# A diffusion layer with experts: modulation in pairs of column blocks, a branch's transfers on another queue, another order of weight slots

## The chip, the cores and the metric

The kernel runs on one core of one Trainium2 chip. The metric is the device time in microseconds (us) of one execution; lower is better.

## The reference

256 latent tokens `x` and 256 context tokens of width 1024 pass one layer. What is computed, cut to the parts that the change touches:

```python
mod_lat = split(silu(c) @ w_mod + b_mod, 6)         # sh1, sc1, g1, sh2, sc2, g2: 1024 each
mod_ctx = split(silu(c_ctx) @ w_mod + b_mod, 6)     # of these only csh1, csc1 are used
h_lat = modulate(rms_norm(x, norm_mix_g), sh1, sc1) # modulate: h * (1 + scale) + shift
h_ctx = modulate(rms_norm(ctx, norm_mix_g), csh1, csc1)
y = token_mixer(h_lat, h_ctx, ...)   # w_in projections, two linear-attention branches, w_out_a, w_out_b, gates, w_out
x = x + g1 * y
h = modulate(rms_norm(x, norm_ffn_g), sh2, sc2)
x = x + g2 * moe_ffn(h, ...)         # each token in 4 of 32 experts; w_gu (1024x2048) and w_down (1024x1024) of each
return rms_norm(x, final_norm_g)
```

All tensors are 32-bit floats. The experts' weights are 32 x 12 MB and are each read once.

## The kernel before, in words

The work falls into four stages. **The start** computes the first two modulation vectors and the normalized inputs (`hT`, split into a rounded part and its rest, and `hF`, unsplit). **The mixer** runs two orders written out by hand, `ORDER1` and `ORDER2` (lines 34 and 35): each word calls one piece (`K`, `Q`, `V`, `P`: projections, `U`, `X`: gated linear attention, `A`, `I`, `B`: gated delta rule, and so on), and a planner orders the instructions of each engine after its own costs. **The tail** (from line 998) multiplies with the rest of `w_out_a`, with `w_out`, adds the residual and computes the router. **The experts** (from line 1323) run one after the other: each takes 12 chunks of 1 MB, 8 of `w_gu` and 4 of `w_down`.

**The other four modulation vectors** (gate 1, shift 2, scale 2, gate 2) are made during `ORDER1`. Each of its 32 words `M1` calls `wmod_next` (line 889) for one block of 128 columns of `w_mod`: two transfers of 256 KB into a ring of three tiles `wm`, eight matmuls in four column groups (each group sums two of the eight row blocks, on its own 32 partitions of the bank `pm`), a copy `mr` of 128x128 out of the bank (VectorE and ScalarE take turns), and one step later `wmod_sum`: a matmul with `mr` as weights and a column `sum4` sums the four groups into `pc`, and one VectorE instruction adds the bias into a column of `mod2`.

**The chunks of the experts' weights** lie in 21 slots, used in turn (`slots`, `mchunk`, `wload`, lines 927 to 962). Most slots are tiles of earlier stages (`hT0`, `ra`, `hT1`, `yh`, `yT`, `hF`, `yl`, `kA`, `x1`), so a slot's first chunk waits for the last reader of the old tile. `prefetch` issues the first ones: the word `C1` of `ORDER2` one chunk each (three), the tail the numbers in `PF` (4 at its begin, then after each merge and each output block), the latter held back by a tiny GpSimd copy that waits for the step's result. The last three of the first round go through GpSimd's queue; all other chunks through SyncE's, in the order of the program, which carries the weights of all projections too.

**A branch** (`beyond`, line 1290) computes experts that got more than 64 tokens. It stands ahead of expert 12, behind the issue of 20 chunks (line 1349); its body has transfers on SyncE's queue. In this run it isn't taken.

**The last expert** weights its result `pd` by the token's share and the gate (`ys`), splits it into two parts and scatters them with matmuls onto the tokens (`py`); then the final norm follows.

Of the kernel before, what the change touches and what calls it, by code (L numbers as in the profile page):

```python
# [20 lines left out]
KT = 8  # L21
# [8 lines left out]
NB1 = 10  # L30
PF = (4, 0, 2, 0, 0, 1, 1, 0, 1, 0, 2, 1, 0)
DN = (0, 2, 1, 3)
HLB = (2, 2)
ORDER1 = "K0 Pq0 K1 Pk0 M1 U0 Pv0 Pv1 Pq1 Pk1 U1 M1 Pv2 M1 X0 M1 M1 M1 R0 M1 M1 K2 Pk2 Q0 M1 M1 Pq2 R1 M1 Pv4 M1 U2 Pq3 T0 M1 Pv3 X1 M1 M1 V0 Pv6 M1 Pv5 M1 T2 M1 T1 R2 M1 M1 Pk3 U3 V3 M1 V1 M1 Pv7 M1 X2 M1 R4 M1 K3 R3 M1 T3 V2 M1 R5 X3 Q1 Q2 R6 M1 M1 Q3 M1 R7 M1 M1"
ORDER2 = "A0 A0 G0 A0 A0 I0 I0 I0 I0 I0 I0 K4 G1 Z0 I0 K5 G3 Z1 G4 K6 G2 Z2 I0 G5 G6 K7 Z3 B0 B0 B0 B0 B0 B0 A1 T4 Q4 B0 A1 V4 Q6 V5 A1 A1 I1 T6 I1 T7 G7 I1 I1 T5 Z4 I1 I1 V6 H0 Q5 H1 Z5 I1 V7 I1 Q7 H2 Z6 B1 Z7 B1 B1 W0 H3 B1 B1 B1 C1 H4 B1 H5 H6 J0 Y0 Y1 Y2 H7 C1 Y3 C1"


@with_exitstack
def hybrid_layer(ctx, tc, x, c, ctxt, c_ctx, w_mod, b_mod, norm_mix_g, norm_ffn_g, w_in, conv_w, a_log_f, a_log_b,
# [307 lines left out]
    T.transpose(pt, GeT.rearrange("p a h c -> p (a h c)"), ident)  # L347
    Gr = cst.tile([128, 128], F32, name="Gr")
    V.tensor_copy(Gr, pt)
# [537 lines left out]
    wms = [0]  # L887

    def wmod_next(n):

        for _ in range(n):
            k, wms[0] = wms[0], wms[0] + 1
            col = 2048 + 128 * k
            if "pD" in gl_static:
                w = wtake(w_mod, col)
                w = w[:, 0:4], w[:, 4:8]
            else:
                w = [ga.tile([128, 4, 128], F32, tag="wm", bufs=3, name=f"wm{k}{i}") for i in range(2)]
                for i in range(2):
                    nc.sync.dma_start(w[i], w_mod[0][512 * i:512 * i + 512, col:col + 128].rearrange("(k p) n -> p k n", p=128))  # L900

            pt = GD([128, 128], f"pm{k}")
            for kt in range(KT):
                r = 32 * (kt % 4)
                T.matmul(pt[r:r + 32], sc[:, kt], w[kt // 4][:, kt % 4], start=kt < 4, stop=kt >= 4)
            mr = lng.tile([128, 256], F32, tag="sq", bufs=2, name=f"mr{k}")[:, 0:128]
            (S.copy if k % 2 else V.tensor_copy)(mr, pt)
            pend.append((k, mr))
            if k:
                wmod_sum()  # L910
            if k == 31:
                wmod_sum()

    pend = []

    def wmod_sum():
        k, mr = pend.pop(0)
        pc = GD([128, 1], f"pc{k}")
        T.matmul(pc, mr, sum4, start=True, stop=True)
        v_, b = (2, 0, 1, 3)[k // 8], k % 8  # L920
        if v_ == 1:
            V.scalar_tensor_tensor(mod2[:, 1, b:b + 1], pc, b1c[:, b:b + 1], vc[:, 72 + b:73 + b], ALU.add, ALU.mult)
        else:
            V.tensor_add(mod2[:, v_, b:b + 1], pc, vc[:, 40 + k:41 + k])


    slots = [("hT0", 0), ("hT0", 1), (big, "ra")]
    nslot = NB1 + 11
    wide = {}
    nch = [0]  # L930

    def mchunk(name):
        pool, tag = slots[nch[0] % nslot]
        nch[0] += 1
# [8 lines left out]
    def wload(e, wgu, wdn, i, after=None):  # L943

        if (e, i) in pre:
            return pre.pop((e, i))
        w = mchunk(f"w{e}_{i}")

# [3 lines left out]
        if i < 8:  # L952
            q.dma_start(w, wgu[128 * i:128 * i + 128, :])
        else:
            r = 256 * DN[i - 8]
            w3, d3 = w.rearrange("p (k n) -> p k n", k=2), wdn[r:r + 256, :].rearrange("(k p) n -> p k n", p=128)
            if (e, i) == (NE - 1, 11):
                for k in range(2):
                    q.dma_start(w3[:, k], d3[:, k])
            else:  # L960
                q.dma_start(w3, d3)
        return w

    def prefetch(n, after=None):

        for _ in range(min(n, len(slots) - nch[0])):
            e, i = divmod(nch[0], 12)
            pre[e, i] = wload(e, w_gu[0, e], w_down[0, e], i, after)
# [107 lines left out]
    S.dma_start(bf[1], b_down[0])  # L1076
    slots += [(big, "hF"), (mwA, "m0"), (big, "yl"), (big, "kA"), (mo, "x1")]
    prefetch(nslot - nch[0])
# [113 lines left out]
    def ffn(e, xe, wts, sel, places_, mid=None, post=None, late=False, last=False):  # L1192
# [54 lines left out]

        oT, pc = places_()
        ys = wk.tile([128, 512], F32, tag="glu", bufs=1, name=f"ys{e}")
        V.scalar_tensor_tensor(ys, pd, pc, grow, ALU.mult, ALU.mult)  # L1250
# [4 lines left out]
        def scatter():  # L1255
            for t in range(2):
                for a in range(2):
                    for hf in range(2):
                        mm(py[t][:, hf], oT[h_[hf], t], yp[a][h_[hf]], start=False, stop=last and a == 1)
        return scatter  # L1260
# [28 lines left out]

    def beyond():  # L1290
        rd = dr.tile([128, 2, 2, NE], F32, name="rd")
        idd = dr.tile([96, NE], BF16, name="idd")
        vmax = nc.values_load(cnt[0:1, NE:NE + 1], min_val=0, max_val=256)
        with tc.If(vmax > CAP):
            nc.sync.dma_start(rd[:, :, 0], pos)
            nc.sync.dma_start(rd[:, :, 1], pr)
            nc.sync.dma_start(idd, id3)

            def piece(src):
                w = wk.tile([128, 512], F32, tag="sig", bufs=1, name="fw")  # L1300
                nc.sync.dma_start(w, src)
                return w

            with tc.For_i(0, NE, 1) as ev:
                ce = nc.values_load(cnt[0:1, bass.ds(ev, 1)], min_val=0, max_val=256)
                for q in range(1, 4):
                    with tc.If(ce > CAP * q):
                        rc = wk.tile([128, 2, 2], F32, tag="rc", bufs=2, name=f"rc{q}")
                        nc.sync.dma_start(rc[:, :, :, None], rd[:, :, :, bass.ds(ev, 1)])
                        sl = wk.tile([96, 1], BF16, tag="sl", bufs=2, name=f"sl{q}")  # L1310
                        nc.sync.dma_start(sl, idd[:, bass.ds(ev, 1)])
                        V.tensor_scalar_add(rc[:, :, 0], rc[:, :, 0], float(-CAP * q))
# [30 lines left out]
    for e in range(NE):  # L1343
        if e == 12:
# [3 lines left out]

            for i in range(20):
                ec, ic = e + i // 12, i % 12  # L1350
                pre[ec, ic] = wload(ec, w_gu[0, ec], w_down[0, ec], ic)
            beyond()
            quad(e)
            place(e)

        def post(e=e):
# [4 lines left out]
            if e + 1 < NE and e + 1 != 12:  # L1361
                if (e + 1) % 4 == 0:
# [3 lines left out]
                     sc_[0], post, e == 0, e == NE - 1)  # L1366
    sc_[0]()


    fg = mchunk("fg")  # L1370
    nc.sync.dma_start(fg[:, 0:D], dap(final_norm_g, 0, [[0, 128], [1, D]]))
    yo = mchunk("yo").rearrange("p (t n) -> p t n", t=2)
    yg = wk.tile([128, 512], F32, tag="aT", name="yg")
# [39 lines left out]
```

## Time and profile before

| | us |
|---|---|
| median of 3 runs | 1624.34 (1623.12 to 1627.99) |
| the profiled execution | 1624.66 |
| its span, first to last instruction | 1622.8 |
| TensorE busy | 1463.0 (90%) |
| VectorE busy | 652.4 (40%) |
| ScalarE busy | 455.4 (28%) |

Times in the rows are us from the span's start unless marked ns. PE is TensorE's matmul, PEld its weight load, DVE VectorE, ACT ScalarE, POOL GpSimd, SP SyncE; a "q" behind the name means the engine's sequencer (waits, branches, issue of transfers). PEclk is the granted share of TensorE's clock. "L905" is line 905. A 32-bit matmul of the program appears as two instructions.

### The profile page before, as it was taken

How to read it: one execution, taken by the hardware profiler on the slowest of the kernel's cores; microseconds unless marked ns; L12 is line 12 of the kernel's file. 1: busy time of each engine (PE TensorE's matmuls, PEld its weight loads, DVE VectorE, ACT ScalarE, POOL GpSimd, SP SyncE). 2: the span in 40 equal slices, each digit the busy share in tenths (PEclk: the TensorE clock that was granted, in tenths of full speed). 3: DMA queues.
4: the chain of work that ended last, by engine and by line, in shares of the span. 5: the costliest groups of instructions: out<-in, count | busy, mean ns of one | idle time of the engine just before them, and what ended most of it. 6: DMA issues, size and time to landing. Idle time of an engine off the chain costs nothing. (4 is left out here: it accounts for less than half of the span.)

```text
span 1622.8 us, 22690 instructions
## 1 busy us (share of the span) xinstructions
PE 1463.0 (90%) x9150; PEld 812.6 (50%) x9151; DVE 652.4 (40%) x1540; ACT 455.4 (28%) x984; POOL 20.6 (1%) x53
## 2 busy tenths in 40 slices
PE   6999999998998898999999987989889889889886
PEld 2777777877886798633434323323223223223221
DVE  4785676795689776511212111111111111111112
ACT  2655455664365544510101000011001011001001
POOL 2000000000000000000000000000000000000000
PEclk9899999999999999999999999999999999999999
DMA  9437454643333539899999999999999999999997
GB/s 292 133 94 196 116 155 127 166 119 104 104 92 97 191 120 339 274 416 417 415 416 417 414 417 373 416 416 416 416 416 418 415 416 417 415 417 416 415 417 295
DMA packets 221934, 491.82 MB, mean 303 GB/s; under 512 B 13106, under 2 KB 150664, under 8 KB 189024
## 3 DMA queue, kind: packets, MB, share of 16 engines
q1 hardware_dynamic: 220096, 485.86, 79.3%
q0 software_dynamic: 1056, 3.46, 0.6%
q8 instruction: 74, 1.21, 0.3%
q10 hardware_dynamic: 672, 0.99, 0.2%
q14 instruction: 36, 0.29, 0.1%
HBM read 489.15 MB, written 1.11 MB: 302 GB/s over the span
## 5 line engine op out<-in xcount | busy, mean ns | idle before, releaser
L1098 PE MATMUL g<-w,xTm 128*64 128x512 f32 x1616 | 375.1, 599 | 36.7 <-DMA w<-in_w_gu_dram 35.1
L1098 PEld LDWEIGHTS g<-w,xTm 128*64 128x64 f32 x1616 | 105.9, 136 | 281.1 <-issue 166.0
L1220 DVE TENSOR_SCALAR glu<-g 128x256 f32<-128x256 f32 x64 | 24.2, 419 | 464.7 <-PE g L1098 464.7
L1098 PE MATMUL pd<-w,aT 128*64 128x512 f32 x864 | 195.8, 597 | 2.0 <-DMA w<-in_w_down_dram 1.8
L203 PE MATMUL pdin_w_in_dram<-hT,hiin_w_in_dram 128*128 128x512 f32 (+1 forms) x704 | 161.1, 366 | 5.6 <-ACT z L809 3.9
L1221 ACT ACTIVATE sig<-glu 128x256 f32<-128x256 f32 x64 | 23.3, 409 | 501.0 <-DVE glu L1220 501.0
L203 PEld LDWEIGHTS pdin_w_in_dram<-hT,hiin_w_in_dram 128*128 128x128 f32 x704 | 115.4, 190 | 29.0 <-issue 6.7
L1250 DVE SCALAR_TENSOR_TENSOR ys<-pd,pcm,grow 128x512 f32<-128x512 f32 x32 | 24.0, 751 | 255.7 <-PE pd L1098 255.7
L1098 PEld LDWEIGHTS pd<-w,aT 128*64 128x64 f32 x864 | 59.7, 137 | 114.5 <-issue 98.4
L1098 PE MATMUL g<-chT,xTm 128*64 128x512 f32 x432 | 102.4, 600 | 12.7 <-DMA chT<-in_w_gu_dram 11.9
L391 DVE SCALAR_TENSOR_TENSOR ra<-ra,cw 128x192 f32<-128x192 f32 (+2 forms) x192 | 90.3, 474 | 13.7 <-ACT ra L385 11.2
L279 PE MATMUL pfin_w_in_dram<-hF,win_w_in_dram 128*128 128x256 f32 x368 | 90.5, 394 | 0.3 <-ACT tgb L358 0.3
L1252 ACT CAST ysig<-ys 128x512 fp32r<-128x512 f32 x32 | 19.8, 618 | 252.1 <-DVE ys L1250 252.1
L203 PE MATMUL pdin_w_in_dram<-hT,loin_w_in_dram 128*128 128x512 f32 (+1 forms) x352 | 83.2, 367 | 2.2 <-DVE loin_w_in_dram L83 2.2
L279 PEld LDWEIGHTS pfin_w_in_dram<-hF,win_w_in_dram 128*128 128x128 f32 x368 | 70.4, 197 | 12.1 <-issue 1.6
L83 DVE TENSOR_TENSOR loin_w_in_dram<-win_w_in_dram,hiin_w_in_dram 128x1024 fp32r<-128x1024 f32 x49 | 59.6, 1219 | 22.0 <-ACT hiin_w_in_dram L82 21.3
L1098 PEld LDWEIGHTS g<-chT,xTm 128*64 128x64 f32 x432 | 27.9, 136 | 77.0 <-issue 40.7
L203 PEld LDWEIGHTS pdin_w_in_dram<-hT,loin_w_in_dram 128*128 128x128 f32 x352 | 59.1, 190 | 14.3 <-DVE loin_w_in_dram L83 3.2
L1231 PE MATMUL pa<-ident,glu 128*128 128x128 f32 x128 | 26.6, 289 | 39.6 <-DVE glu L1224 38.0
L82 ACT CAST hiin_w_in_dram<-win_w_in_dram 128x1024 fp32r<-128x1024 f32 x49 | 51.2, 1045 | 16.6 <-DMA win_w_in_dram<-in_w_in_dram 11.2
L1098 PE MATMUL pxm<-ohm,xp 128*128 128x256 f32 x256 | 36.1, 297 | 6.1 <-DVE ohm L1139 4.4
L1098 PEld LDWEIGHTS pxm<-ohm,xp 128*128 128x128 f32 x256 | 33.2, 200 | 13.5 <-PE g L1098 4.9
(489 smaller groups left out, 1927.1 us busy)
## 6 DMA issues: line engine op xcount, KB each, us to landing
w<-in_w_gu_dram SPq DMA_DIRECT2D x200, 1024.0 KB, 20.0
w<-in_w_down_dram SPq DMA_DIRECT2D x106, 1024.0 KB, 20.1
chT<-in_w_gu_dram SPq DMA_DIRECT2D x54, 1024.0 KB, 20.0
win_w_in_dram<-in_w_in_dram SPq DMA_DIRECT2D x72, 512.0 KB, 4.0
chT<-in_w_down_dram SPq DMA_DIRECT2D x20, 1024.0 KB, 20.1
wm<-in_w_mod_dram SPq DMA_DIRECT2D x64, 256.0 KB, 3.5
wm<-in_w_mod_dram SPq DMA_DIRECT2D x16, 512.0 KB, 12.6
win_w_out_b_dram<-in_w_out_b_dram SPq DMA_DIRECT2D x8, 512.0 KB, 4.1
```

The source lines that it names most:

```text
L82: S.copy(hi, src)
L83: V.tensor_sub(lo, src, hi)
L203: T.matmul(p if n == 256 else p.rearrange("p (a b) -> p a b", a=2), hl[i][:, kt], r, start=i + a + kt == 0, stop=a == 1 and kt == KT - 1)
L279: T.matmul(p, w[:, kt], act[:, kt], start=kt == 0, stop=kt == KT - 1)
L391: V.scalar_tensor_tensor(al[:, r0:r1], raw[:, r0 + y - 1:r1 + y - 1, x_:x_ + 64], wc(y, x_), al[:, r0:r1], ALU.mult, ALU.add)
L1098: return inorder(T.matmul(*args, **kw))
L1220: V.tensor_scalar_min(gl_[:, cs], pg[0][:, cs], 7.0)
L1221: sig = S.activation(sg_[:, cs], gl_[:, cs], AF.Sigmoid, scale=1.702)
L1231: T.transpose(pt[:, a], gl_[:, 256 * c_ + 128 * a:256 * c_ + 128 * a + 128], ident))
L1250: V.scalar_tensor_tensor(ys, pd, pc, grow, ALU.mult, ALU.mult)
L1252: S.copy(yp[0], ys)
```

## The change

1. `wmod_next` takes two column blocks a call: 16 words `M1` instead of 32, at nearly the same places of `ORDER1` (the one ahead of `U0` goes). Each call has four transfers, 16 matmuls into one bank of 256 columns, one VectorE transpose in blocks of 32x32 out of the bank and a copy of every 32nd column into `modT`. After the last call four matmuls with a wider `sum4` sum all 32 blocks at once, and five VectorE instructions make `mod2`.
2. The slots have another order: `hF` first, then `ra`, then `hT0`; four words `C1` in `ORDER2` instead of three, the first of them earlier; `PF` begins 1, 2, 2 instead of 4, 0, 2.
3. The branch's transfers are issued by GpSimd; ten chunks instead of 20 are issued ahead of it, and the load of the count it compares is tied behind the tenth.
4. The last expert weights, splits and scatters its result in two halves of 256 columns.

```diff
-PF = (4, 0, 2, 0, 0, 1, 1, 0, 1, 0, 2, 1, 0)
+PF = (1, 2, 2, 0, 0, 1, 1, 0, 1, 0, 2, 1, 0)
...
-    sum4 = cst.tile([128, 1], F32, name="sum4")
-    V.tensor_reduce(sum4, ident[:, 0:128:32], AX.X, ALU.add)
+    sum4 = cst.tile([128, 32], F32, name="sum4")
+    V.tensor_reduce(sum4, ident.rearrange("p (g j) -> p j g", g=4), AX.X, ALU.add)
...
+            pt = GD([128, 256], f"pm{k}")
+            for j in range(2):
+                col = 2048 + 256 * k + 128 * j
                 for i in range(2):
+                    w = ga.tile([128, 4, 128], F32, tag="wm", bufs=3, name=f"wm{k}{j}{i}")
+                    nc.sync.dma_start(w, w_mod[0][512 * i:512 * i + 512, col:col + 128].rearrange("(k p) n -> p k n", p=128))
+                    for kt in range(4):
+                        T.matmul(pt[32 * kt:32 * kt + 32, 128 * j:128 * j + 128], sc[:, 4 * i + kt], w[:, kt],
+                                 start=i == 0, stop=i == 1)
+            mr = lng.tile([128, 256], F32, tag="sq", bufs=2, name=f"mr{k}")
+            V.transpose(mr, pt)
+            V.tensor_copy(modT[:, k], mr[:, 0:256:32])
+        if wms[0] == 16:
+            pc = GD([128, 32], "pc")
+            mv = modT.rearrange("p k b -> p (k b)").rearrange("p (b q) -> p q b", q=4)
+            for q in range(4):
+                T.matmul(pc[32 * q:32 * q + 32], sum4, mv[:, q], start=True, stop=True)
...
-    slots = [("hT0", 0), ("hT0", 1), (big, "ra")]
+    slots = [(big, "hF"), (big, "ra"), ("hT0", 0), ("hT0", 1)]
...
+    first = [0, 2, 3, 1] + list(range(4, nslot))
...
+        if last:
+            for c_ in range(2):
+                cs = slice(256 * c_, 256 * c_ + 256)
+                ys = wk.tile([128, 256], F32, tag="xT", bufs=4, name=f"ys{e}{c_}")
+                V.scalar_tensor_tensor(ys, pd[:, cs], pc, grow[:, cs], ALU.mult, ALU.mult)
...
+                S.copy(yp[0], ys)
+                V.tensor_sub(yp[1], ys, yp[0])
+                for a in range(2):
+                    for t in range(2):
+                        for hf in range(2):
+                            mm(py[t][:, hf, cs], oT[h_[hf], t], yp[a][h_[hf]], start=False, stop=c_ + a == 2)
+            return None
...
-        vmax = nc.values_load(cnt[0:1, NE:NE + 1], min_val=0, max_val=256)
+        with tc.issue_after(behind.ins):
+            vmax = nc.values_load(cnt[0:1, NE:NE + 1], min_val=0, max_val=256)
         with tc.If(vmax > CAP):
-            nc.sync.dma_start(rd[:, :, 0], pos)
+            G.dma_start(rd[:, :, 0], pos)
...
-            for i in range(20):
+            for i in range(10):
                 ec, ic = e + i // 12, i % 12
                 pre[ec, ic] = wload(ec, w_gu[0, ec], w_down[0, ec], ic)
-            beyond()
+            beyond(dmas[ec, ic])
```

## Rows read from the trace of the kernel before

**Rows 1.** The page: the span, and what the DMA moved in each of 40 equal slices of it (40.6 us each).

```profile
span 1622.8 us, 22690 instructions
...
GB/s 292 133 94 196 116 155 127 166 119 104 104 92 97 191 120 339 274 416 417 415 416 417 414 417 373 416 416 416 416 416 418 415 416 417 415 417 416 415 417 295
```

**Rows 2.** The stages: busy us (and instructions) of PE, PEld, DVE, ACT and POOL in each stretch, then the granted clock, the DMA's share and GB/s.

```profile
73.00:314.00 241.00, 237.27 (x1705) 183.82 (x1704) 169.67 (x408) 132.93 (x278) 2.08 (x5) 0.99 0.51 140
...
591.00:674.00 83.00, 75.29 (x566) 68.30 (x566) 51.89 (x115) 38.12 (x87) 3.54 (x9) 0.98 0.84 284
...
710.00:945.00 235.00, 222.82 (x1210) 86.45 (x1210) 45.18 (x109) 26.63 (x62) 0.00 (x0) 0.99 1.02 416
...
1003.00:1016.00 13.00, 8.24 (x58) 7.04 (x59) 3.42 (x6) 2.52 (x5) 0.00 (x0) 0.74 0.73 286
1016.00:1600.00 584.00, 512.96 (x2658) 180.61 (x2659) 94.97 (x231) 55.85 (x131) 0.00 (x0) 1.00 1.02 416
```

**Rows 3.** The chain of waits that ended last, around 1060 us: start, duration, what.

```profile
1063.79 20.07 DMA w<-in_w_gu_dram
```

**Rows 4.** Groups of instructions by line and shape, 60 to 600 us: count, busy us, mean ns of one, idle before.

```profile
L905 PE MATMUL pm<-wm,sc 128*32 128x128 f32 x512 | 24.1, 282 | 1.5 <-DMA wm<-in_w_mod_dram 1.3
...
L919 PE MATMUL pc<-sum,mr 128*128 128x1 f32 x64 | 11.4, 248 | 0.0
...
L907 DVE COPY mr<-pm 128x128 f32<-128x128 f32 x16 | 4.6, 286 | 9.3 <-PE pm L905 9.3
...
L924 DVE TENSOR_TENSOR mod<-pc,vc 128x1 f32<-128x1 f32 x24 | 3.7, 156 | 11.0 <-PE pc L919 10.9
...
L645 DVE STREAM_TRANSPOSE XD<-X 128x1024 f32<-128x1024 f32 x2 | 4.1, 2073 | 0.1
```

**Rows 5.** TensorE's matmuls in order of time, 100 to 130 us: start, duration, line, tiles, count.

```profile
107.30 0.65 PE L905 MATMUL pm<-wm,sc 128*32 128x128 f32 x16
107.88 0.38 PE L919 MATMUL pc<-sum,mr 128*128 128x1 f32 x2
108.19 0.33 PE L515 MATMUL pa<-f 128*64 128x64 f32 x2
...
129.15 0.43 PE L905 MATMUL pm<-wm,sc 128*32 128x128 f32 x8
129.51 0.38 PE L919 MATMUL pc<-sum,mr 128*128 128x1 f32 x2
129.75 0.48 PE L203 MATMUL pdin_w_in_dram<-hT,hiin_w_in_dram 128*128 128x512 f32 x1
```

**Rows 6.** All waits of TensorE's matmuls, 73 to 314 us: us in total, times, longest.

```profile
PE pdin_w_in_dram L203 <- DVE loin_w_in_dram L83: 2.2, 1, 2.2
PE pm L905 <- DMA wm<-in_w_mod_dram: 1.3, 2, 0.7
```

**Rows 7.** SyncE's transfers of the modulation weights around 130 us.

```profile
124.62 8.12 SPq L900 DMA_DIRECT2D wm<-in_w_mod_dram  x7
```

**Rows 8.** TensorE in the tail: the products with the last part of w_out_a, and the first product of the first expert.

```profile
622.41 0.64 PE L858 MATMUL pa<-ya,hia 128*128 128x256 f32 x4
625.48 0.74 PE L858 MATMUL pa<-ya,hia 128*128 128x256 f32 x4 [2.42 <-ACT hia L82]
626.74 0.82 PE L858 MATMUL pa<-ya,loa 128*128 128x256 f32 x4 [0.52 <-DVE loa L83]
...
673.85 1.08 PE L1098 MATMUL g<-chT,xTm 128*64 128x512 f32 x4
```

**Rows 9.** SyncE's issue of the fourth part of w_out_a in the tail, and the landing times of the eight transfers of its line.

```profile
610.12 0.41 SPq L845 DMA_DIRECT2D in_w_out_a_dram<-in_w_out_a_dram  x1
...
DMA to landing us min/median/max: 3.4/4.6/13.6
```

**Rows 10.** The stretch behind that wait: columns as in rows 2.

```profile
625.00:630.00 5.00, 4.01 (x21) 3.80 (x22) 3.41 (x5) 1.82 (x3) 0.00 (x0) 0.73 1.03 377
```

**Rows 11.** The branch's line: sequencer instructions, count, ns (min/median/max), first and last start.

```profile
L1294 SPq EVENT_SEMAPHORE  x9: 17/17/17, 994.1 to 1006.9; - x9
...
L1294 SPq COMPARE_BRANCH  x1: 50/50/50, 988.9 to 988.9; - x1
...
L1294 PEldq COMPARE_BRANCH  x1: 3692/3692/3692, 1004.3 to 1004.3; - x1
```

**Rows 12.** SyncE around the branch (a line covers transfers issued in a row), and from the page the usual time from issue to landing.

```profile
1007.02 0.81 SPq L953 DMA_DIRECT2D chT<-in_w_gu_dram  x2
...
w<-in_w_gu_dram SPq DMA_DIRECT2D x200, 1024.0 KB, 20.0
```

**Rows 13.** The hole in the stream: columns as in rows 2.

```profile
1000.00:1005.00 5.00, 2.80 (x16) 0.84 (x12) 1.44 (x2) 0.62 (x1) 0.00 (x0) 1.00 0.83 344
1005.00:1010.00 5.00, 0.99 (x4) 1.02 (x5) 0.69 (x1) 0.00 (x0) 0.00 (x0) 0.61 0.43 138
```

**Rows 14.** The end: two pieces of the chain of waits, and from the page the mean of VectorE's 128x512 weighting and of an instruction of 128x256.

```profile
1611.94 0.76 DVE ys L1250
...
1614.72 1.12 ACT yo L1376 x2
...
L1220 DVE TENSOR_SCALAR glu<-g 128x256 f32<-128x256 f32 x64 | 24.2, 419 | 464.7 <-PE g L1098 464.7
...
L1250 DVE SCALAR_TENSOR_TENSOR ys<-pd,pcm,grow 128x512 f32<-128x512 f32 x32 | 24.0, 751 | 255.7 <-PE pd L1098 255.7
```

More of the change, by code (lines that the diff above doesn't have):

```diff
@@ L903, in wmod_next @@
[L903 to L924, printed above, removed]
@@ new lines, in wmod_next @@
+            mr = lng.tile([128, 256], F32, tag="sq", bufs=2, name=f"mr{k}")
[6 more added lines that the diff above has]
+                T.matmul(pc[32 * q:32 * q + 32], sum4, mv[:, q], start=True, stop=True)
+            for i, v_ in enumerate((2, 0, 1, 3)):
+                c8 = slice(8 * i, 8 * i + 8)
+                if v_ == 1:
+                    V.tensor_add(mod2[:, 1], pc[:, c8], b1c)
+                    V.tensor_mul(mod2[:, 1], mod2[:, 1], vc[:, 72:80])
+                else:
+                    V.tensor_add(mod2[:, v_], pc[:, c8], vc[:, 40 + 8 * i:48 + 8 * i])
@@ L930, in hybrid_layer, with mchunk @@
     nch = [0]
-    def mchunk(name):
-        pool, tag = slots[nch[0] % nslot]
-        nch[0] += 1
+    first = [0, 2, 3, 1] + list(range(4, nslot))
+    dmas = {}
+    def mchunk(name, c):
+        pool, tag = slots[c % nslot]
         if pool in ("hT0", "hT1"):
@@ L966, in prefetch @@
         for _ in range(min(n, len(slots) - nch[0])):
-            e, i = divmod(nch[0], 12)
+            e, i = divmod(first[nch[0]], 12)
+            nch[0] += 1
             pre[e, i] = wload(e, w_gu[0, e], w_down[0, e], i, after)
@@ L1076, in hybrid_layer @@
     S.dma_start(bf[1], b_down[0])
-    slots += [(big, "hF"), (mwA, "m0"), (big, "yl"), (big, "kA"), (mo, "x1")]
+    slots += [(mwA, "m0"), (big, "yl"), (big, "kA"), (mo, "x1")]
     prefetch(nslot - nch[0])
@@ L1248, in ffn @@
         oT, pc = places_()
+        if last:
[3 more added lines that the diff above has]
+                V.scalar_tensor_tensor(ys, pd[:, cs], pc, grow[:, cs], ALU.mult, ALU.mult)
+                yp = [wk.tile([128, 256], F32R, tag=tag, bufs=4 if tag == "xT" else 1, name=f"y{tag}{e}{c_}")
+                      for tag in (("sig", "lin"), ("xT", "xT"))[c_]]
+                S.copy(yp[0], ys)
[5 more added lines that the diff above has]
+            return None
         ys = wk.tile([128, 512], F32, tag="glu", bufs=1, name=f"ys{e}")
@@ L1258, in scatter @@
                     for hf in range(2):
-                        mm(py[t][:, hf], oT[h_[hf], t], yp[a][h_[hf]], start=False, stop=last and a == 1)
+                        mm(py[t][:, hf], oT[h_[hf], t], yp[a][h_[hf]], start=False, stop=False)
         return scatter
@@ L1287, in gate2, with beyond @@
             S.copy(grow[h_[hf]], pt[h_[hf]])
[L1290 removed]
+    def beyond(behind):
         rd = dr.tile([128, 2, 2, NE], F32, name="rd")
         idd = dr.tile([96, NE], BF16, name="idd")
[L1293 removed]
+        with tc.issue_after(behind.ins):
+            vmax = nc.values_load(cnt[0:1, NE:NE + 1], min_val=0, max_val=256)
         with tc.If(vmax > CAP):
[L1295 to L1297 removed]
+            G.dma_start(rd[:, :, 0], pos)
+            G.dma_start(rd[:, :, 1], pr)
+            G.dma_start(idd, id3)
             def piece(src):
                 w = wk.tile([128, 512], F32, tag="sig", bufs=1, name="fw")
[L1301 removed]
+                G.dma_start(w, src)
                 return w
```

30 lines of the change are left out of this document (11 added, 19 removed).

## The prediction

> **What bounds the kernel now.** I read the page's head first: 1622.8 us of span, and a transfer rate that stands near 416 GB/s from about 690 us to the end, with one dip to 373 GB/s in the slice that begins at 974 us [rows 1]. The busy time by stage splits the span [rows 2]. From 73 to 314 us TensorE is busy 237.27 of 241 us while the DMA moves 140 GB/s: TensorE bounds the first stage, in which all the modulation work of this change lies. From 591 to 674 us (the output projections) it is still busiest, 75.29 of 83 us. From 710 us to 1600 the DMA is full at 416 GB/s, except from 1003 to 1016 us, where it gave 286. The chain of waits agrees: up to 1063.79 us it runs through TensorE, and then from one weight transfer of 20 us to the next until the last expert [rows 3]. So two things make the end: when the first expert starts (673.85 us [rows 8]; everything before is TensorE's), and holes in the stream behind it. Each chunk is 1.05 MB, 2.52 us at 416 GB/s. A us gained before 674 moves the end by a us, if as many chunks have landed by then. Counting in the code, before: 3 in the second order and 4+2+6 in the tail; after: 4 and 1+2+2+6. Both are 15, and the rest follows the same releases.
>
> **Modulation, the same part.** 32 column blocks, 64 transfers of 256 KB and 256 matmuls stay; four of them side by side in four column groups, as before. The matmul group is 512 instructions and 24.1 us of busy time [rows 4]; I cost its change at 0.
>
> **Modulation, what goes.** 32 summing matmuls, each with a 128x128 weight load, shown as 64 instructions and 11.4 us of busy time [rows 4]. What one costs TensorE is its distance to the next start: 108.19-107.88 = 0.31 us, or 129.75-129.51 = 0.24 us [rows 5]. I take 0.24: 32 x 0.24 = 7.7 us. The new sum is four matmuls at the end, 4 x 0.24 = 1.0 us. Net -6.7 us, on the path, since TensorE's waits of the whole stage are 2.2 and 1.3 us [rows 6]: there is nearly no idle time into which the gain could fall. Ends: -9 (0.31 each, and the wait for transfers gone) and +2 (the 64 quarter blocks of matmuls, which now may be split oftener. A block of 16 takes 107.88-107.30 = 0.58 us, a block of 8 takes 129.51-129.15 = 0.36, so 64 blocks of 8 would take 23.0 against 32 x 0.58 = 18.6, some 4 us more than whole blocks, and eat most of the gain). I stay at -6.7, because the groups of before were split in the same way already.
>
> **Modulation, VectorE.** Before, 16 copies of 286 ns and 24 additions of 156 ns (and 8 of a similar kind); the other 16 copies were ScalarE's. After, 16 transposes of 128x256 and 16 short copies. No transpose of that shape is in the trace; one of 128x1024 takes 2073 ns [rows 4], a quarter is 0.52 us, and a copy of half the width is 0.29. With 0.15 for the short copy: 16 x 0.67 = 10.7 us against 4.6+3.7+1.2 = 9.5. VectorE is busy 169.67 of 241 us [rows 2]; I cost it at 0. If every bit of the difference were on the path it would be 1 us; a transpose of 0.29 us would give 4 us back to VectorE, which again nobody waits for.
>
> **Earlier and later chunks.** Chunk 0 now goes to the slot of the normalized input, which is free once the whole projections are done, so four chunks pass before 600 us, while the DMA has room (92 to 191 GB/s in the slices from 400 to 600 us [rows 1]). Behind that the first load of the tail falls from 4 chunks to 1, and two each follow the first and second merge. Before, the fourth output weight was issued at 610.12 us behind these chunks, and the slowest of this group landed after 13.6 us against 4.6 as median [rows 9]. [...] With 1 chunk ahead instead of 4 the weight lands some 9 us earlier, 3 x 2.52 us and more. I take back 2.42+0.52 and 0.27 x 2 of the slower clock: -3.5. Ends: -5 (all the slow clock, 1.35 us, and what waits behind), and +2.5 (one chunk more in front of a later output weight).
>
> **The branch.** At the branch SyncE compares once at 988.9 us and then works through nine semaphore instructions from 994.1 to 1006.9 [rows 11]; its next weight transfer goes out at 1007.02 [rows 12]. I read these as waits in which it lets its whole queue land, since the branch's body holds transfers of its own. With 20.0 us from issue to landing (eight chunks in flight) [rows 12] the queue bridges most of these 18 us, and the hole is what is left: (416-344)/416 x 5 + (416-138)/416 x 5 = 0.9 + 3.3 = 4.2 us [rows 13]. After, the body's transfers are GpSimd's, which has none in flight that anyone needs then. I take -4.2. Ends: 0 (the hole stays) and -4.3. TensorE's own branch (3692 ns) [rows 11] stays and shows nowhere: between 1004 and 1016 us five chunks land and eight are in flight, and 21 slots leave eight more, 20 us, before the ring is full. The 10 loads ahead of the branch instead of 20 keep SyncE's comparison in front of slots that are still in use.
>
> **The last expert.** From the start of the weighting at 1611.94 to the first square at 1614.72 are 2.78 us [rows 14]. In halves, each step of 128x512 (751 ns) is one of 128x256 (419 ns) [rows 14], and the halves overlap on two engines: two weightings 0.8, cast 0.4, difference 0.4, matmuls 0.4, gaps 0.2 make 2.2. -0.5 us on the path; ends 0 and -0.8.
>
> **Sum.** -6.7 - 3.5 - 4.2 - 0.5 = -14.9 us. The profiled execution took 1624.66 us (span 1622.8, 1.9 around it), the median shown is 1624.34: 0.3 apart, which I neglect. 1624.66 - 14.9 = 1609.8; I say 1610.
>
> **Rivals.**
> 1. The hole stays or moves (chance 0.10): SyncE still stops at the branch, because something behind it needs GpSimd's or TensorE's side. For it: TensorE too compares at this branch [rows 11], so each engine may have its part in it. Against: in the body SyncE's own transfers are what its nine waits are for. 1610 + 4.2 = 1614.
> 2. The hole was worth nothing (0.03), since the stream runs faster behind it and makes the 4.2 us up: 1614 too. Against it, the stream ran at 416 GB/s before the hole and at 416 after it [rows 2]. [...]
> 3. The first stage gives little (0.12): the matmul blocks are split finer, or TensorE then waits on the transposes or on ScalarE's splits. Then -6.7 becomes 0: 1616.5.
> 4. Slower (0.06): weight transfers in fours over a ring of three. The fourth can only go out when TensorE has used the first, and what stands behind it in SyncE's queue, the projection's weights, waits with it. The trace shows seven such transfers issued over 8.12 us, 1.16 us apart [rows 7], and TensorE kept up by working on projections between them. If the order now puts the four quarters of a step together, TensorE waits for the transfers, up to three such spacings or 3.5 us a step. It decides from 14.9/16 = 0.93 us of standing a step on; at 2 us a step, 32 us: 1642.
> 5. Nothing moves (0.07): another order of instructions takes back what the sums save, 1620 to 1625.
>
> The forecast itself has 0.62, with its own range of 1606 to 1613.5.
>
> **How the numbers follow.** The low end adds the far ends: 6.7 becomes 9, 3.5 becomes 5: 1606, less 2 for what follows them: 1604. The high end takes in rivals 1 to 3 and stops where rival 5 begins: 1619. A measurement of this kernel can tell 0.3% from no change, 4.9 us: faster means under 1619.4. the forecast and rivals 1 to 3 all lie there: 0.87. Rival 5 is the same: 0.07. Slower is rival 4: 0.06.
>
> **What would show it.** The small sums gone and the first stage ending 6 to 7 us earlier; no wait of over 1 us on an output weight near 620 us; the first expert's first product some 10 us earlier than 674; no slice below 410 GB/s between 700 us and the end, and SyncE's weight transfers unbroken at the branch; the last weighting in two halves. I am wrong if TensorE shows waits for modulation transfers of over 15 us in sum, if fewer chunks than before have landed when the first expert starts, or if the dip is still there.

## The result and the profile after

The changed kernel takes 1611.78 us (median of 6 runs, 1610.31 to 1616.60) where the kernel before takes 1625.16 beside it: a ratio of 0.992, with a 95% interval of 0.9903 to 0.9938, or 13.0 us less (10.1 to 15.8). Forecast were 1610. Below, a gain in us is always 1625 x (ratio - 1) with its interval, and a profiled execution is named as such: single executions of one kernel lie 6 us apart here and up to 12 in the runs below, so two profiles tell where time goes, and only the medians tell how much.

The page of the changed kernel, against [rows 1]:

```profile
span 1609.4 us, 22554 instructions
...
GB/s 298 118 108 209 142 109 143 177 131 106 79 107 104 184 158 319 334 417 414 416 417 415 416 417 414 415 417 416 415 417 417 416 416 416 415 418 416 415 417 247
```

The dip to 373 is gone: from the 18th slice to the last but one no slice is below 414. The stages of the changed kernel, columns as in [rows 2], each stretch ending where the work of the old one now ends:

```profile
73.00:308.00 235.00, 228.43 (x1645) 174.23 (x1644) 168.66 (x392) 127.62 (x261) 2.45 (x4) 0.99 0.51 144
578.00:660.00 82.00, 75.62 (x562) 67.93 (x560) 51.20 (x114) 38.13 (x86) 1.96 (x11) 0.96 0.84 286
710.00:945.00 235.00, 221.94 (x1188) 84.33 (x1184) 42.22 (x100) 24.78 (x57) 0.00 (x0) 0.99 1.02 416
1003.00:1016.00 13.00, 12.83 (x78) 7.55 (x79) 2.08 (x5) 2.06 (x4) 0.00 (x0) 0.89 1.02 410
```

The stretch at the branch moves 410 GB/s instead of 286 (the changed kernel's branch comes at 992.5 us, and none of the six windows of 5 us from 985 to 1015 us moves less than 405), and the full stream is as fast as before, 416. The tail (578 to 660) takes about as long as before (591 to 674).

The modulation's groups in the changed kernel, 60 to 600 us, against [rows 4] (TensorE's first, then VectorE's):

```profile
L902 PE MATMUL pm<-wm,sc 128*32 128x128 f32 x512 | 24.9, 286 | 4.8 <-DMA wm<-in_w_mod_dram 4.5
...
L912 PE MATMUL pc<-modT,sum 128*32 128x32 f32 x8 | 0.3, 229 | 0.2 <-DVE modT L907 0.2
...
L906 DVE STREAM_TRANSPOSE mr<-pm 128x256 f32<-128x256 f32 x16 | 7.2, 448 | 11.8 <-PE pm L902 11.8
L907 DVE COPY modT<-mr 128x8 f32<-128x8 f32 x16 | 3.1, 197 | 0.2
```

The 64 instructions of the sums are now 8. But the idle time ahead of the `pm` group rose from 1.5 to 4.8 us: TensorE waits for the modulation's transfers, which it did for 1.3 us before [rows 6].

**Where the 13 us are.** The same instruction in the two profiled executions starts earlier by 2.6 us at the first small product behind the first modulation vectors (41.23 to 38.63 us), by 3.7 at 72 us, ahead of the first modulation block of this stage (72.03 to 68.30), by 6.1 at the last modulation matmul (311.80 to 305.66), by 10.0 in the middle of the mixer (448.30 to 438.26), by 13.3 at the mixer's end, by 13.8 at the first expert's first product (673.85 to 660.02), by some 17 at the chunks behind the branch, by 15.7 when the last chunk lands (1610.08 to 1594.34), by 14.0 at the last weighting (1611.94 to 1597.91), and by 13.4 at the end of the span. So some time is gained at the very start, where nothing of the change runs, some is gained between 312 and 590 us, where of the change only chunks are issued, and some is lost between the branch and the end. The experiments have to tell these apart.

The start first, in windows of 5 us, columns as in [rows 2]. The kernel before:

```profile
35.00:40.00 5.00, 3.65 (x12) 1.07 (x12) 1.53 (x4) 1.04 (x1) 0.00 (x0) 0.68 0.62 144
40.00:45.00 5.00, 3.64 (x13) 2.72 (x13) 3.56 (x10) 2.93 (x6) 0.00 (x0) 0.50 0.40 102
45.00:50.00 5.00, 5.00 (x13) 3.83 (x13) 4.70 (x12) 2.05 (x4) 0.86 (x3) 0.50 0.40 111
```

The changed kernel, the same windows:

```profile
35.00:40.00 5.00, 3.31 (x18) 1.88 (x18) 2.51 (x8) 1.66 (x3) 0.00 (x0) 1.00 0.80 193
40.00:45.00 5.00, 3.04 (x10) 2.45 (x11) 5.00 (x14) 4.37 (x8) 0.00 (x0) 0.82 0.52 147
45.00:50.00 5.00, 5.00 (x23) 3.99 (x21) 3.48 (x8) 1.05 (x1) 0.86 (x3) 0.84 0.56 148
```

Before, the clock stood at the lower of the two levels that both traces record (0.50 and 1.00) from 40 to 50 us; after, its means are 0.82 and 0.84. This is no gain of the change: the profile of the run with the modulation part alone has the low clock there too (0.50 and 0.54) and starts that product at 41.24, and that of the run with the branch part alone starts it at 38.62. It differs between these executions.

The end has such a difference too. Some 3 us ahead of the landing of the last chunk, first in the kernel before, then in the changed one:

```profile
1606.00:1608.00 2.00, 2.00 (x12) 0.70 (x10) 0.00 (x0) 0.00 (x0) 0.00 (x0) 1.00 0.68 272
```

```profile
1590.00:1592.00 2.00, 2.00 (x6) 0.47 (x4) 0.00 (x0) 0.00 (x0) 0.00 (x0) 0.50 0.52 211
```

At 0.50 TensorE has 6 matmuls in these 2 us instead of 12 and falls behind, and the last weighting starts 3.6 us behind the landing of the last chunk instead of 1.9. In both kernels TensorE had been busy for only 0.4 of 2 us, 4 us before these windows. Six of the 14 profiles show the lower clock here (mean 0.66 to 0.75 in the last 5 us ahead of that landing, and 3.4 to 3.6 us to the weighting): the changed kernel, the modulation alone, the chunks alone and, of the runs further below, the queue alone, the idle matmuls and the single blocks. The others have 1.00 and 1.9 us. So 1.7 us of what the changed kernel's profile loses at the end are this clock. What decides it is open.

### The profile page after: what moved, and what is told of

It reads as the page before. It is cut to its first block, busy times and chain, and to the rows that moved or that the text cites. A ratio compares the mean times of both kernels' runs of the same rounds, so it can differ in the third digit from the quotient of the medians.

```text
span 1609.4 us, 22554 instructions
## 1 busy us (share of the span) xinstructions
PE 1454.4 (90%) x9102; PEld 802.3 (50%) x9103; DVE 654.5 (41%) x1531; ACT 451.5 (28%) x969; POOL 19.3 (1%) x55
## 5 line engine op out<-in xcount | busy, mean ns | idle before, releaser
L1097 PE MATMUL g<-w,xTm 128*64 128x512 f32 x1688 | 392.2, 599 | 37.5 <-DMA w<-in_w_gu_dram 35.4
L1097 PEld LDWEIGHTS g<-w,xTm 128*64 128x64 f32 x1688 | 110.4, 136 | 289.9 <-issue 171.1
L1097 PE MATMUL pd<-w,aT 128*64 128x512 f32 x792 | 180.7, 604 | 1.2 <-DMA w<-in_w_down_dram 1.2
L1097 PEld LDWEIGHTS pd<-w,aT 128*64 128x64 f32 x792 | 56.0, 139 | 109.9 <-issue 100.4
L1097 PE MATMUL g<-chT,xTm 128*64 128x512 f32 x360 | 83.8, 597 | 6.9 <-DMA chT<-in_w_gu_dram 6.6
L1097 PE MATMUL pd<-chT,aT 128*64 128x512 f32 x232 | 56.3, 620 | 0.0
L1097 PEld LDWEIGHTS g<-chT,xTm 128*64 128x64 f32 x360 | 24.0, 136 | 60.3 <-issue 38.9
```

Of the source, the lines that this page charges most:

```text
L1097: return inorder(T.matmul(*args, **kw))
```

## The experiments

**One part at a time.** Four kernels, each the kernel before with one part of the change (its hunks of the diff and nothing else).

The modulation alone:

```diff
-                T.matmul(pt[r:r + 32], sc[:, kt], w[kt // 4][:, kt % 4], start=kt < 4, stop=kt >= 4)
...
+            V.transpose(mr, pt)
+            V.tensor_copy(modT[:, k], mr[:, 0:256:32])
...
```

> The kernel before with the modulation part alone (pairs of column blocks, the transpose, one sum at the end, the new ORDER1). My prediction: the 32 sums go, -6.7 us, so about 1618 beside 1625 for the kernel before, with the first stage about 6 us shorter, and nothing else moved. Rival (another order of instructions and a better clock made the gain seen in the first stage, not the sums): 1623 to 1626, and a first stage within 2 us of before.

Measured: 1617.35, ratio 0.9948 (0.9931 to 0.9965): -8.4 us (-11.2 to -5.7). As predicted, rather more. The profiled execution, at 1625.09 the longest of its six, lost part of it to this:

```profile
PE pm L902 <- DMA wm<-in_w_mod_dram: 7.8, 8, 2.4
```

At the last modulation matmul this profile is no earlier than the kernel before (312.52 against 311.80 us), so it doesn't show where the 8.4 us of the median come from.

The branch alone:

```diff
-        vmax = nc.values_load(cnt[0:1, NE:NE + 1], min_val=0, max_val=256)
+        with tc.issue_after(behind.ins):
+            vmax = nc.values_load(cnt[0:1, NE:NE + 1], min_val=0, max_val=256)
...
-            nc.sync.dma_start(rd[:, :, 0], pos)
+            G.dma_start(rd[:, :, 0], pos)
...
-            for i in range(20):
+            for i in range(10):
```

> The kernel before with the branch part alone (its transfers on GpSimd's queue, ten chunks ahead of it, the load of the count tied behind the tenth). My prediction: the hole of 4.2 us in the stream closes, so about 1621 beside 1625, and the stretch from 1003 to 1016 us moves over 400 GB/s. Rival (the stream makes the hole up behind it, or something else bounds the end): 1624 to 1626 although the hole is closed.

Measured: 1621.94, ratio 0.9974 (0.9959 to 0.9989): -4.2 us (-6.7 to -1.8). In its profile a chunk that landed 3.7 us later than in the kernel before ahead of the branch lands 0.3 us earlier behind it, 4.0 us of stream won back. The last chunk lands 0.8 us later than in the kernel before, so 2.9 us of the 4.0 reach the end. The stretch is full:

```profile
1003.00:1016.00 13.00, 4.50 (x23) 2.21 (x22) 2.13 (x3) 0.62 (x1) 0.00 (x0) 0.74 1.01 417
```

The chunks alone:

```diff
-    slots = [("hT0", 0), ("hT0", 1), (big, "ra")]
+    slots = [(big, "hF"), (big, "ra"), ("hT0", 0), ("hT0", 1)]
...
-PF = (4, 0, 2, 0, 0, 1, 1, 0, 1, 0, 2, 1, 0)
+PF = (1, 2, 2, 0, 0, 1, 1, 0, 1, 0, 2, 1, 0)
```

> The kernel before with the chunk part alone (slots in another order, four chunks in ORDER2, PF 1, 2, 2). My prediction: -3.5 us, 1621.5, the first expert's first product near 670 us. Rival, from the trace of the changed kernel: the wait on a part of w_out_a goes, but a new wait of some 2 us on a split of w_out and a lower clock behind it give it back: 1624 to 1625, the first product at 673 to 674.

Measured: 1623.55, ratio 0.9990 (0.9978 to 1.0001): -1.6 us (-3.6 to +0.2), between the two expectations and nearer to the rival; by the time alone the -3.5 is not excluded. In its profile the tail gains 1.5 us (0.19 later than before at 591 us, 1.28 earlier at 672).

The halves alone:

```diff
+        if last:
+            for c_ in range(2):
+                cs = slice(256 * c_, 256 * c_ + 256)
+                ys = wk.tile([128, 256], F32, tag="xT", bufs=4, name=f"ys{e}{c_}")
...
```

> The kernel before with the last expert's halves alone. My prediction: -0.5 us, from the start of the last weighting to the first square 2.3 us instead of 2.78. Rival, from the trace of the changed kernel: 2.7 us to the first square, and then ScalarE takes both squares back to back ahead of the root, so that from the first square to the end of the span it is 8.8 instead of 8.1 us: no gain or 0.5 us lost, 1625 to 1626.

Measured: 1625.08, ratio 1.0002 (0.9992 to 1.0013): +0.3 us (-1.3 to +2.1). The weighting starts at 1613.31 in its profile; ScalarE's end:

```profile
1615.69 1.02 ACT L1389 ACTIVATE yo<-py 128x1024 f32<-128x1024 f32 x1 [1.07 <-PE py L1098]
...
1616.71 1.01 ACT L1389 ACTIVATE yo<-py 128x1024 f32<-128x1024 f32 x1
...
1617.70 0.47 ACT L1390 ACTIVATE ss<-ss,cols 128x1 f32<-128x1 f32 x2
```

To the first square it is 2.38 us instead of 2.78: 0.4 of the 0.5 that the halves were to bring. But both squares now come first (probably since with the halves both groups of tokens are finished at the same time), and the first logarithm follows 2.01 us after the first square's start instead of 1.15 (before: square at 1614.72, logarithm at 1615.87). From the first square to the end of the span it is 8.7 us instead of 8.0.

The four add up to -13.9 us, the whole change measured -13.0: within the intervals, some 2 us to either side for each, nothing shows that the parts depend on one another, and the modulation and the branch are nearly all of it.

**Are the sums what the modulation gained?** Two kernels from the kernel before: the sums done twice, and the new order alone.

```diff
         T.matmul(pc, mr, sum4, start=True, stop=True)
+        T.matmul(pc, mr, sum4, start=True, stop=True)
```

> The kernel before with each of the 32 summing matmuls of the modulation done twice, into the same place. By my price (0.24 us each, all of it on TensorE's path) 7.7 us slower, 1633 beside 1625.5; with the dearer row (0.31) 9.9, 1635.5. Rival (the sums lie beside waits and cost nothing): within 2 us of before.

Measured: 1627.54, ratio 1.0011 (0.9996 to 1.0027): +1.8 us (-0.6 to +4.4). The time does not show the price of 7.7, though the trace shows about that where the sums are done. TensorE in order of time, in the kernel with the sums twice:

```profile
101.15 0.38 PE L919 MATMUL pc<-sum,mr 128*128 128x1 f32 x2
101.39 0.36 PE L920 MATMUL pc<-sum,mr 128*128 128x1 f32 x2
101.62 0.71 PE L203 MATMUL pdin_w_in_dram<-hT,hiin_w_in_dram 128*128 128x512 f32 x2
```

The second sum takes 0.23 us to the next start (8.0 in all), and at 323 us this kernel stands 8.4 us behind the one before. At 390 it is 3.7, at 570 3.1. Something between 340 and 390 us and again near 530 gives 5 us back.

```diff
-ORDER1 = "K0 Pq0 K1 Pk0 M1 U0 ... M1 Pv2 M1 X0 M1 M1 M1 R0 ..."
+ORDER1 = "K0 Pq0 K1 Pk0 U0 ... M1 M1 Pv2 X0 M1 M1 M1 M1 R0 ..."
```

> The kernel before with the changed kernel's ORDER1, each of its 16 modulation words taken as two of the old ones: old transfers, copies and sums, at the new places. If the sums make the gain, this one has no gain: TensorE's waits for modulation weights rise from 1.3 to 4 us or more in the first stage, since two words' transfers now meet a ring of three, and the time is 1626 to 1631. Rival (the order makes the gain): 1617 to 1621.

Measured: 1627.12, ratio 1.0018 (1.0001 to 1.0036): +2.9 us (0.2 to 5.9). The order is not the gain. The wait for the modulation's transfers did not rise, though (1.3 us in its profile), so the reason given for the loss is not shown.

**The stalls.** What gives back is seen in TensorE's waits in the stretch of the small matmuls (blocks of 32x32, lines 657 to 671), 355 to 545 us. "issue" is a stall for which the profile shows no cause. The kernel before:

```profile
PE pw L671 <- issue: 2.1, 1, 2.1
PE pw L670 <- issue: 2.0, 1, 2.0
...
PE pw L667 <- issue: 1.9, 1, 1.9
```

The kernel with the sums twice:

```profile
PE pw L669 <- issue: 1.3, 1, 1.3
...
PE pw L668 <- issue: 0.5, 1, 0.5
```

And the changed kernel:

```profile
PE pw L670 <- issue: 1.5, 1, 1.5
...
PE pw L666 <- issue: 0.7, 1, 0.7
```

6.0 us, 1.8 and 2.2. I numbered TensorE's records in each trace in order of their start (matmuls, weight loads, its sequencer's). The stalls of the kernel before stand at records 4802, 5058 and 7361; with the sums twice at 5057 and 7362; in the changed kernel at 4802 and 7105; with the order alone at 4802, 5058 and 7361. The distances are 256 and multiples of it (one record missing here and there). So what counts is which instructions stand at every 256th place: the changed kernel, with 110 records fewer ahead of this stretch, and the kernel with 128 more both have one fewer of these places well inside the fastest matmuls (32x32, 203 ns each, the shortest of this stretch; a place right at their begin, record 7105 of the kernel before, shows no stall). To test it alone, 32 matmuls that nobody reads, at a place where TensorE is idle (4.42 us ahead of its matmul at 10.87 us in the kernel before):

```diff
     V.tensor_copy(vcc, pt)
+    dm = TP([128, 128], "dm")
+    for n in range(32):
+        T.matmul(dm[0:32, n:n + 1], ident[:, 0:32], ident[:, 0:1], start=True, stop=True)
```

> The kernel before with 32 idle matmuls of one column near 6 us, where TensorE waits for data. They compute nothing that is used. In all traces so far TensorE's stalls with no cause in the profile ('issue', at the small matmuls of lines 666 to 671) stand at the same count of its instructions, 256 apart, whatever the kernel and the time; the kernel before has three of them, 6.0 us in sum, the kernel with the sums twice (128 more records) 1.8, the changed one (some 110 fewer) 2.2. If the count sets them, 128 records more at a free place bring them to about 1.8 us, and the kernel gets about 4 us faster by doing more: 1621. Rival (the stalls belong to the data or the time, not to the count): 6 us of stalls and 1625, or some tenths more.

Measured: 1619.73, ratio 0.9971 (0.9956 to 0.9985): -4.7 us (-7.1 to -2.4), from doing more. Its waits in the same stretch:

```profile
PE pw L672 <- issue: 1.1, 1, 1.1
...
PE pw L671 <- issue: 0.9, 1, 0.9
```

They stand at records 5058 and 7361: 2.0 us in sum instead of 6.0. Its profile starts the experts 6.7 us earlier than the kernel before (667.20 us); 4.0 of these come at the stalls, and 2.7 are there at 72 us (69.36 instead of 72.03). One profile can't tell whether the idle matmuls help the start, or whether this is its clock again (0.85 from 45 to 50 us); the last run below has 56 of them, and its clock there is 0.53.

What TensorE waits for in a stall is in the traces too. The page of the kernel before lists, among the DMA queues, one for instructions (packets, MB):

```profile
q8 instruction: 74, 1.21, 0.3%
```

Each of its packets is 16 KB, and 74 of them for 18491 records make one for 250. In the kernel before the packets nearest to the three stalls come in at 374.89 to 375.86, 378.17 to 379.05 and 532.26 to 533.31 us, and the stalls end at 377.12, 380.57 and 534.69: 1.3, 1.5 and 1.4 us behind the packet. All 37 stalls of over 0.25 us in this stretch of the 14 traces end so, 1.2 to 1.6 us behind the end of such a packet, long ones and short ones. I read this as TensorE standing still there until its next instructions have come. Of the 13 places 256 records apart that the kernel before has in this stretch, three show such a stall; over the 14 traces one takes 0.3 to 2.6 us.

It also bears on the price of the sums: this kernel and the one with the sums twice have the same 128 records more and nearly the same stalls, and differ by the 32 further sums: +1.8 against -4.7, 6.5 us, where each has an interval of some 2.5 to either side. That agrees with 7.7.

**The branch's two edits.** The queue alone (20 chunks and no tie), and the ten chunks alone (SyncE's queue):

```diff
-            nc.sync.dma_start(rd[:, :, 0], pos)
+            G.dma_start(rd[:, :, 0], pos)
...
```

> The kernel before with the branch's transfers on GpSimd's queue, but still 20 chunks issued ahead of the branch and the load of the count not tied. If SyncE stops because the body holds transfers of its own, the hole is gone with this edit alone: 1621, over 400 GB/s from 1003 to 1016 us. Rival (the ten chunks and the tie are what keeps the stream whole): the dip stays, 1624 to 1626.

```diff
-            for i in range(20):
+            for i in range(10):
```

> The kernel before with ten chunks ahead of the branch instead of 20, its transfers still on SyncE's queue. If SyncE's stop comes from its own transfers in the body, the hole stays, and is no shorter than before (1625 or up to 3 us more, since fewer chunks are in flight when it begins). Rival (the ten chunks close it): 1621.

Measured: the queue alone 1623.85, ratio 0.9989 (0.9974 to 1.0004), -1.8 us (-4.2 to +0.6); the ten chunks alone 1624.87, ratio 1.0009 (0.9995 to 1.0024). The hole, first with the queue moved, then with ten chunks:

```profile
1003.00:1016.00 13.00, 4.85 (x24) 1.44 (x20) 1.91 (x3) 0.62 (x1) 0.00 (x0) 0.79 1.01 416
```

```profile
1003.00:1016.00 13.00, 8.43 (x61) 7.32 (x62) 3.20 (x7) 2.63 (x5) 0.00 (x0) 0.74 0.71 280
```

The queue closes it, the ten chunks do nothing to it (SyncE works through the same nine semaphore instructions, from 993.7 to 1006.5 us). In the profile of the queue alone the stream gains the same 4.0 us at the branch (chunks 5.04 us later ahead of it, 1.1 behind it, and 2.2 at the last one). That the median shows only 1.8 is within its interval; whether the ten chunks add something to the moved queue can't be told from these times.

**Can the new waits go?** Two kernels from the changed one. First single blocks at the old places, with the one sum at the end kept:

```diff
-            pt = GD([128, 256], f"pm{k}")
-            for j in range(2):
...
+            col = 2048 + 128 * k
+            pt = GD([128, 128], f"pm{k}")
...
-            V.tensor_copy(modT[:, k], mr[:, 0:256:32])
+            V.tensor_copy(modT[:, k // 2, 4 * (k % 2):4 * (k % 2) + 4], mr[:, 0:128:32])
```

> The changed kernel with its modulation in single blocks of 128 columns at the places of the old ORDER1 (two transfers a word, a transpose of 128x128 each, the one sum at the end kept). If the four transfers of a pair against the ring of three make TensorE's new waits (4.5 us in the changed kernel's first stage, 7.8 in the run with the modulation alone), they fall to 1 to 2 us and the time to about 1608.5 beside 1611.8. Rival (the waits come from the weights' rate, or VectorE's 16 further transposes take the gain): 1611 to 1613.

Measured: 1610.73, ratio to the kernel before 0.9904 (0.9884 to 0.9925): -15.6 us (-18.9 to -12.2). Its waits for modulation weights, 73 to 314 us:

```profile
PE pm L900 <- DMA wm<-in_w_mod_dram: 1.5, 3, 0.6
```

1.5 instead of 4.5, and the last modulation matmul comes at 300.84 instead of 305.66. But the records now stand 13 further ahead of the small matmuls, and the stalls are 1.9, 0.8 and 1.7 us (records 4801, 7106, 7362). By the medians it can't be told from the changed kernel.

Then the tail and the end:

```diff
-PF = (1, 2, 2, 0, 0, 1, 1, 0, 1, 0, 2, 1, 0)
+PF = (1, 2, 0, 1, 1, 1, 1, 0, 1, 0, 2, 1, 0)
...
-        S.activation(yo[:, t], py[t].rearrange("p a n -> p (a n)"), AF.Square, accum_out=ss2[:, 0, t:t + 1])
...
+        inorder(S.activation(yo[:, t], py[t].rearrange("p a n -> p (a n)"), AF.Square, accum_out=ss2[:, 0, t:t + 1]))
...
```

> The changed kernel with two edits: PF 1, 2, 0, 1, 1 instead of 1, 2, 2, 0, 0 (the two chunks behind the second merge go behind the third and fourth), and the last squares, logarithms and exponentials kept in the order of the program. If the chunks ahead of the w_out weights make the wait of 1.9 us on their split, it goes, and the first expert's first product comes 2 us earlier against the mixer's end; if the order of ScalarE makes the end 0.7 us longer, first square to end of span falls from 8.8 to 8.1. Together 1609 beside 1611.8. Rival (other waits take their place): 1611 to 1612.

Measured: 1609.97, ratio 0.9910 (0.9894 to 0.9926): -14.6 us (-17.2 to -12.0). In the changed kernel the tail waits on the split of a part of `w_out`, whose transfers were issued at 609.0 and 610.0 us behind two chunks of 608.1 and 608.5:

```profile
621.63 1.21 PE L203 MATMUL pdt<-yTh,hit 128*128 128x256 f32 x8 [1.92 <-ACT hit L82]
```

With the chunks moved, of the same wait is left, 590 to 680 us:

```profile
PE pdt L203 <- ACT hit L82: 0.3, 1, 0.3
```

and from the mixer's end to the first expert's first product the tail gains 2.4 us on the changed kernel. That half is as expected. The end is a miss: ScalarE now stands still between the two groups of tokens.

```profile
1601.51 0.37 ACTq L1398 DMA_DIRECT2D out_dram<-yo  x1
1601.93 1.02 ACT L1389 ACTIVATE yo<-py 128x1024 f32<-128x1024 f32 x1 [1.90 <-DVE yo L1395]
```

Held to the program's order, ScalarE issues the first output transfer ahead of the second square, and waits there for VectorE. From the first square to the end of the span it is 10.2 us instead of 8.8.

Last, all of it with the end put right and the stalls' places chosen:

```diff
+    for n in range(24):
+        T.matmul(dm[0:32, n:n + 1], ident[:, 0:32], ident[:, 0:1], start=True, stop=True)
...
+        if t == 0:
+            inorder(S.activation(ss2[:, 1, 0:1], ss2[:, 0, 0:1], AF.Ln, bias=epsc, scale=1.0 / D))
...
```

> The changed kernel with what the runs point to: the modulation in single blocks at the old places, PF 1, 2, 0, 1, 1, 56 idle matmuls of one column at the start (224 records, so that the 256th ones fall where the run with the idle matmuls had them), and the last squares in the order of the kernel before (square, logarithm and exponential of the first half of the tokens, then those of the second). Each by what its own run showed against the changed kernel: waits for modulation weights 1.5 instead of 4.5 us, the split's wait 0.3 instead of 1.9, stalls 2 instead of 2.6 us, the end 0.4 us better than in the kernel before: about 5 us together, 1606 beside 1611.8 and 1625. Rival (they take each other's gain back, as the stalls did in the run with single blocks): 1609 to 1612.

Measured: 1609.27 (1607.86 to 1610.29), ratio 0.9912 (0.9885 to 0.9939): -14.3 us (-18.7 to -9.9). It beats the kernel before, and its median is 2.5 us below the changed kernel's, but by the ratios the two can't be told apart. In its profile the stalls are 1.6 us, the split's wait 0.3, and the first square to the end 8.1 instead of 8.8, as expected. But from the start of the last weighting to the end it takes 10.8 us, as in the kernel before: the 0.4 us of the halves are not there (2.67 us to the first square). The wait for modulation weights is not as expected either:

```profile
PE pm L906 <- DMA wm<-in_w_mod_dram: 4.9, 6, 1.8
```

4.9 us, with the same order and transfers that had 1.5 in the run with single blocks. Why is open; the wait is not set by the pairs alone.

## Why the prediction was right, step by step

**What bounds the kernel** held: what TensorE saved ahead of 590 us came off the start of the experts, and most of what the stream saved at the branch stayed saved: chunks land 12.9 us earlier ahead of it, 16.9 behind it, and the last one 15.7, so 2.8 us of 4.0. Why the rest goes, though the rate is 416 GB/s in both kernels, is open.

**Modulation, -6.7.** The part alone measured -8.4. The step on the sums was right: 64 instructions took 7.8 us from start to start, the new 8 take 0.23. But the total is right, by luck, through two terms that I did not have and that nearly cancel in the changed kernel's profile. "TensorE's waits of the whole stage" did not stay: the wait for transfers rose from 1.3 to 4.5 us, +3.2. And the stalls at every 256th record fell from 6.0 to 2.2, -3.8, at a place 60 us behind the last instruction of the change. They stood in the trace of before as waits of up to 2.1 us with no cause named, and I had looked at TensorE's waits only from 73 to 314 us [rows 6]. In the profile of the modulation alone they don't cancel (+6.5 and -3.4). The quarter blocks of matmuls that I had feared are 21.6 us from start to start instead of 20.8.

**VectorE, 0.** The transpose measured 448 ns, against an estimate of 0.52 us, and the short copy 197 against 150. That nobody waits for them was not tried by itself; the run with 32 narrower transposes shows no loss by them.

**Chunks, -3.5.** This is the step that failed. "I take back 2.42+0.52", TensorE's two waits at the products with the last part of `w_out_a` [rows 8]: the first went, but two chunks behind the second merge put a transfer of `w_out` late, 1.92 us, and the end "+2.5 (one chunk more in front of a later output weight)" was the better half of my bounds. 0.52 is still there in the changed kernel. The 0.54 for the slower clock, twice what 0.73 [rows 10] lacks to 1.00, is shown by no run: the changed kernel's clock is 0.85 and 0.81 from 620 to 630 us, behind the new wait, where it was 0.73 for 5 us behind the old one (1.00 from 625 to 627 us, 0.50 from 628 to 630). The part alone measured -1.6, in the profile of the changed kernel the tail gains 0.55.

**Branch, -4.2.** Measured -4.2, with 4.0 in the stream at the branch and 2.9 left at the last chunk; the median's interval holds both. The reading of SyncE's nine instructions as waits for its own queue, because the body held its transfers, is shown by the queue alone closing the hole and the ten chunks leaving it; and the last of the nine, at 1006.9 us, follows the landing of the last chunk issued ahead of the branch, at 1006.81. The sentence on the ten loads was needless: with 20 the hole closes too. TensorE's own branch took 6.1 us instead of 3.7. VectorE waited for it (7.0 us, 4.6 before), the stream, at 405 GB/s or more, did not:

```profile
L1308 SPq COMPARE_BRANCH  x1: 50/50/50, 992.5 to 992.5; - x1
L1308 SPq EVENT_SEMAPHORE  x1: 17/17/17, 992.7 to 992.7; - x1
L1308 PEldq COMPARE_BRANCH  x1: 6083/6083/6083, 992.9 to 992.9; - x1
```

SyncE's nine semaphore instructions [rows 11] are one.

**Last expert, -0.5.** 0.4 to the first square in the run with the halves alone, near what I worked out, and 0.1 in the changed kernel (2.67 us); but I stopped the sum at that square, and behind it the new order of ScalarE costs 0.7: together nothing, or a little lost. ScalarE in the changed kernel:

```profile
1600.58 1.02 ACT L1389 ACTIVATE yo<-py 128x1024 f32<-128x1024 f32 x1 [1.10 <-PE py L1097]
1601.50 0.20 ACT L1389 ACTIVATION_READ_ACCUMULATOR yo<-py 128x1 f32 x1
1601.59 1.01 ACT L1389 ACTIVATE yo<-py 128x1024 f32<-128x1024 f32 x1
...
1602.59 0.47 ACT L1390 ACTIVATE ss<-ss,cols 128x1 f32<-128x1 f32 x2
```

**Sum.** -14.9 was forecast and -13.0 measured. The chunks and the last expert brought 2.7 us less than their terms and the modulation 1.7 more, so the total is nearer than its terms: that part is luck.

**The rivals.** 1 fell: the hole is closed. 2 fell: of the 4 us most stayed gained, at 416 GB/s on both sides of the hole. 3 fell by the time. The wait of 4 is there, with 3.2 us more in sum, 0.2 a step, where it decides from 0.93 on; that the transfers in fours make it is not shown, since the new order alone had 1.3 us and the last run, with two transfers a word, 4.9. 5 was right in kind, other instructions do take back and give, but they gave.

**What was to show it.** The sums are gone, the stream and the last weighting as told. "The first stage 6 to 7 us earlier" reads 6.1, but 3.7 of these were there before its first modulation block, from the start's clock; more came later, 3.8 with the stalls. "No wait of over 1 us on an output weight near 620 us" was wrong by the 1.92. The first product came 13.8 us earlier instead of 10. Of this and of the 4.0 at the branch, 0.9 went ahead of the branch, 1.2 between it and the last chunk, and 2.4 behind that, through the clock in the last products (1.7) and ScalarE's order (0.7).

## What to carry to other kernels

Before costing a change from the waits of its own stage, read the waits with no cause named in all stages: a change in the number of instructions moves them, here by 4 us at a place that it doesn't touch. A branch whose body held transfers of the queue that feeds the kernel stopped that queue here although it wasn't taken (286 GB/s from 1003 to 1016 us, 416 with the queue moved); give the body a queue that nobody needs. Where a step is moved out of a queue's or an engine's way, work the sum out to the last instruction of the program, not to the first one that comes earlier.

## What was not expected

TensorE stalls at places a multiple of 256 of its records apart, where these lie well inside the fastest of its small matmuls, of 203 ns (once right behind them): 1.9 to 2.1 us each in the kernel before, each ending 1.2 to 1.6 us behind a 16 KB packet of the instruction queue; and 32 idle matmuls near 6 us, where it stood idle for 4.42 us anyway, make the kernel 4.7 us faster. The clock at 40 to 50 us differs between executions of the same code (0.50 to 0.86 in windows of 5 us), and the first small product behind it started between 38.6 and 42.2 us in these profiles. TensorE's compare at a branch not taken took 3.69 us in the kernel before and 3.43 with the ten chunks alone, where the body's transfers are on SyncE's queue, and 6.08, 5.95 and 6.01 in the changed kernel, the branch alone and the queue alone, where they are on GpSimd's; SyncE's took 50 ns in all five. An instruction packet comes in during it, too: in the kernel before at 1005.26 to 1006.52 us in a compare of 1004.33 to 1008.02, in the changed kernel at 996.34 to 997.50 in one of 992.94 to 999.03, so both end 1.5 us behind it.
